# Masks and sums of a state scan moved from GpSimd to ScalarE and VectorE, and a depthwise convolution that begins at the first tile of queries

## The chip, the cores and the metric

The kernel runs on one core of a Trainium2 chip, as one program. The core has TensorE (PE in the profile; its weight loads are PEld), VectorE (DVE), ScalarE (ACT), GpSimd (POOL) and SyncE (SP, which here issues DMAs). The metric is the device time of one execution in microseconds (us), less being better. Before the change the median of three runs is 3319.76 us, from 3314.33 to 3324.03. All arithmetic is float32; the large products are made as three products of a high and a low part (fp32r), so that each costs three matmuls.

## The reference

One inference step of a hybrid backbone with two layers. The tokens are 128 of a context and 1024 of a noisy latent, 1152 in all, each of 1024 numbers. Per layer one input projection feeds three mixers that stand side by side: attention with compressed keys (8 heads), a bidirectional state scan (4 heads of 64, chunks of 128 tokens), and a convolution module. Then come the output projection, and a gated feed-forward part.

```python
h = rmsnorm(x, g_mix) * (1 + sc1) + sh1
comb = h @ w_in                            # [ q_c | ckv | krope | z x B C dt | conv a b ]

# state scan, both directions, chunk by chunk
acs = cumsum(dt * a)
seg = exp(where(lower, acs[l] - acs[s], -inf))
y_diag = einsum('bclhn,bcshn,bhcls,bcshp->bclhp', cf, bf, seg, x * dt)
y_off = einsum('bclhn,cbhpn,bhcl->bclhp', cf, h_in, exp(acs))
ssm = rmsnorm((y_fwd + y_bwd + ssd_d * xs) * silu(z))

# convolution module
g = a * sigmoid(b)
g = dwconv(g, cm_conv_w) + cm_conv_b       # 31 taps, each channel by itself
conv = silu(layernorm(g))                  # over the channels

attn = softmax(q @ k.T * scale) @ v
x = x + g1 * (concat([attn, ssm, conv]) @ w_out)
x = x + g2 * (silu(h2 @ w_gate) * (h2 @ w_up)) @ w_down
```

## The kernel before

Tokens are worked in three chunks of 384, which are nine tiles of 128. Within a layer the stages follow each other in this order: the projection of the scan's inputs; the scan's states (`ssd_states`); the convolution module's projection and gate (`conv_in`, which writes `glu`, 256 channels in two tiles of 128 by 1167 useful columns); the token-major projection of q_c, ckv and krope (`token_major`, with `token_tail` for norms, rotary keys and transposes); the scan's outputs (`ssd_out`); `latents`, `prep_k`, `prep_v`, `prep_r` and `prep_q`, which make keys, values and queries; attention; the output projection; the feed-forward part. A string of letters (L737) interleaves `conv_in`, `ssd_states`, `token_major`, `ssd_out` and `latents`, so their instructions lie among each other.

The program names no order of its own between engines beyond that: a scheduler reorders the instructions when the program is built, and then every engine works off its queue in a fixed order and waits where an operand or a buffer isn't ready. What stands behind a waiting instruction on its engine waits too.

`ssd_out` (L475 to L553) makes nine chunks' outputs. For a chunk, two masks of 128 by 128 (`M_in`, one for each direction) are multiplied by the four heads' columns of dt (L492, two GpSimd instructions of 128 by 512 in tiles of the tag E), added on VectorE (L78), and multiplied by the product of C and B from PSUM (L501). The exponents come from four masked tiles `mv` (L508; three buffers), two from the high part of dt·a on VectorE and two from its low part on GpSimd, of which TensorE makes `db` (L510); ScalarE takes the exponential (L512). Then come TensorE's `yb` (L523), the product D·x (L526) and, from chunk 1 on, two sums of `y` with the states' part `of` (L78). These three are on GpSimd for chunks 0 to 4 and on VectorE for chunks 5 to 8.

The long convolution (`conv_taps`, L863 to L873) is all on GpSimd: for each of two accumulators a first tap (L868) and 30 further taps, each a product (L871) and a sum (L78) of 128 by 1167. It needs only `glu`. A one-column copy on GpSimd (L517) from the scan's last exponentials into `ct`, the taps' scratch tile, stands ahead of them, so that they begin when chunk 8 of the scan has its exponentials. In the program text three taps are drawn per tile of queries.

Attention goes over four pairs of heads and nine tiles. From the 26th tile on, one step of `conv_norm` is drawn per tile: TensorE sums the two accumulators over channels (L881), VectorE centres (L885), ScalarE squares (L889), TensorE sums squares (L896), and so on. `load_w` brings a weight tile, rounds it to its high part on ScalarE (L84) and makes the low part `wl` on GpSimd (L81) in one of four buffers; those of the output projection stand in GpSimd's queue among layer 1's taps.

Of the kernel before, what the change touches and what calls it, by code (L numbers as in the profile page):

```python
# [53 lines left out]
def build(tc, nc, ap, dbg=None):  # L54
# [99 lines left out]
    def spread(r, dg, tag):  # L154
        """[128 tokens, 3] -> a PSUM bank with r of each token on every partition."""
        dg = dg.rearrange("p (a b) -> p a b", a=3)
        V.tensor_mul(dg, ident.unsqueeze(1).to_broadcast([128, 3, 128]),
                     r.unsqueeze(2).to_broadcast([128, 3, 128]))
        b = bank(tag)
        PE.matmul(b[:, :CH], ones, dg.rearrange("p a b -> p (a b)"), start=True, stop=True)  # L160
        return b

# [1 line left out]
    KO = (0, 4, 1, 5, 2, 6, 3, 7)  # L164

    def adas(rounds, stage=None, ahead=2):
        """128 columns of each of a round's four quarters at a time; loads run ahead of the products"""
        stage = stage or wp
        steps = [(l, r, q, k) for l, r in rounds for q in range(4) for k in range(0, KD, 2)]
        loads = []  # L170
        m = None
        for n in range(len(steps) + ahead):
            if n < len(steps):
                l, r, q, k = steps[n]
                loads.append(stage.tile([128, 1024], F32, tag="ws", name="ws", bufs=ahead + 1))
                Q.dma_start(loads[-1], ap["w_ada"][l, r, q, k // 2])
            if n >= ahead:
                l, r, q, k = steps[n - ahead]
                st = loads.pop(0)
                if k == 0:  # L180
                    m = sm.tile([128, 128], F32, tag="ms", name="ms", bufs=2)
                b = bank("A")
                for kk in range(2):
                    for j in range(4):
                        o = 512 * kk + 128 * j
                        PE.matmul(b[32 * j:32 * j + 32, :128], cond[:, k + kk, :], st[:, o:o + 128],
                                  start=kk == 0, stop=kk == 1)
                if k:
                    add_to(V, m, b[:, :128], m)
                else:  # L190
                    copy(m, b[:, :128])
                if k == KD - 2:
                    ada_end(l, r, q, m)
            yield
# [25 lines left out]
    def norm_r(x, p, sqs=None):  # L220
        """1 / rms of the chunk's tokens on every partition; sqs: room for all squares, summed on TensorE"""
# [79 lines left out]
    for c in (1, 2):  # L301
        # a load that would only hold up the modulation's goes behind them
        V.tensor_copy(X[c][:, 0, 0:1], modT[0][:, c + 1, 0:1])
        Q.dma_start(X[c], ap["xT"][:, c])
# [5 lines left out]
    for l in range(L):  # L310
# [6 lines left out]
        def h_terms(c, w):  # L317
            """stationary weights [k, cols], moving h chunk"""
            hh, hl = H[c]
            return [(w[0][:, 128 * k:128 * k + 128], w[1][:, 128 * k:128 * k + 128], hh[:, k], hl[:, k])  # L320
                    for k in KO]

        # ================= in projection: x, B, C of the scan =================
# [17 lines left out]
        for c in range(NC3):  # L341
# [34 lines left out]
        # lowest: what the attention's first tiles can take over soonest  # L376
# [6 lines left out]
        # ================= state-space scan =================  # L383
        # dt = softplus(.), log1p(e) = 2 atanh(e / (2 + e))
# [89 lines left out]
        def ssd_out():  # L474
# [12 lines left out]
            for c in range(9):  # L487
                o = xcol(c)
                # dt of the pairs of tokens in each direction's range
                W = [tmp(512, "E", 4).rearrange("p (h t) -> p h t", h=4) for _ in range(2)]  # L490
                for d in range(2):
                    G.tensor_tensor(W[d], M_in[d].unsqueeze(1).to_broadcast([128, 4, 128]),  # L492
                                    v4(dt)[:, d, c, :].unsqueeze(2).to_broadcast([128, 4, 128]), ALU.mult)
                add_to(V, W[0], W[1], W[0])
                W = W[0]
# [7 lines left out]
                # a direction's exponents are 0 outside of its range  # L503
                db = bank("A")
                for d in range(2):
                    for i, (dd, en) in enumerate(((dah, V), (dal, G))):
                        mv = tmp(512, "mv", 3, F32R).rearrange("p (h t) -> p h t", h=4)
                        en.tensor_tensor(mv, M_in[d].unsqueeze(1).to_broadcast([128, 4, 128]),  # L508
                                        v4(dd.bitcast(F32))[:, d, c, :].unsqueeze(2).to_broadcast([128, 4, 128]), ALU.mult)
                        PE.matmul(db, M_sr[d], mv.rearrange("p h t -> p (h t)"), start=d + i == 0, stop=d + i == 2)  # L510
# [3 lines left out]
                if c == 8:  # L514
                    # the long convolution's products would hold up the scan on this engine
                    lat["ct"] = r4t("ct")
                    G.tensor_copy(lat["ct"][:, 0:1], E[:, 0, 0:1])  # L517
# [7 lines left out]
                e = G if c < 5 else V  # L525
                e.tensor_tensor(y.rearrange("p (h q) -> p h q", h=4), xst[:, c].rearrange("p (h q) -> p h q", h=4),  # L526
                                dsum.unsqueeze(2).to_broadcast([128, 4, 64]), ALU.mult)
                V.tensor_add(y, y, yb[:, :256])
                if c:
# [7 lines left out]
                    for d in range(2):  # L537
                        add_to(e, y, of[:, d].rearrange("p h q -> p (h q)"), y)
# [16 lines left out]
        # ================= in projection: conv module =================  # L555
# [28 lines left out]
        def latent(c):  # L584
            """chunk c's query latent (high and low part, halves), key latent (high and low part), rotary key"""
# [35 lines left out]
        def token_tail(c, tns, ss):  # L621
            # rotary key part
# [57 lines left out]
        def latents():  # L680
            # cached keys
# [60 lines left out]
        # ================= attention =================  # L742
# [42 lines left out]
        class Tile_:  # L785
            """one tile of queries of a pair of heads"""
# [6 lines left out]
            def scores(self, j):  # L793
                """exp of a head's scores, less their maximum, and the sums"""
# [27 lines left out]
            def attend(self):  # L822
# [25 lines left out]
                # divide by the sums  # L848
# [14 lines left out]
        def conv_taps():  # L863
            ct = lat["ct"]
# [10 lines left out]
        def conv_norm(c):  # L875
            """layer norm over channels and silu of chunk c"""
# [68 lines left out]
        # ================= out projection, residual, norm 2 =================  # L945
# [36 lines left out]
        # ================= feed-forward =================  # L982
# [21 lines left out]
        def finish(c):  # L1004
            """what follows the layer for chunk c: the next layer's first norm, or the final norm"""
# [13 lines left out]
            # nothing is left to overlap with  # L1019
# [7 lines left out]
        def apply(c, rs):  # L1027
            """the final norm's scale for chunk c"""
# [70 lines left out]
def layouts(i):  # L1099
    """the arrays of setup_inputs, laid out for the program"""  # L1100
# [80 lines left out]
```

## Time and profile before

| what | value |
|---|---|
| median of 3 runs | 3319.76 us |
| profiled execution, its span from first to last instruction | 3325.1 us |
| granted TensorE clock, mean over the span | 0.967 |
| TensorE busy | 3123.8 us (94%) |
| VectorE busy | 1856.9 us (56%) |
| ScalarE busy | 1081.1 us (33%) |
| GpSimd busy | 1183.7 us (36%) |

The profile gives of the profiled execution its span alone, no time of its own; the span lies 5.3 us above the median of the three runs and 1.1 us above the longest of them. Busy times are sums over instructions. A matmul's end is modelled, so a busy TensorE need not be at its peak; of the clock, 1.0 is full speed. In a row of the timeline, "[48.58 <-ACT wh L84]" is the engine's idle time before the instruction and what ended it.

### The profile page before, as it was taken

The page shows a single profiled execution, that of the slowest core. Times are in us where ns is not written, and L with a number is a line of the kernel's source. Part 1 is how long each engine was busy: PE and PEld are TensorE (multiplying, and loading weights), DVE is VectorE, ACT ScalarE, POOL GpSimd, SP SyncE. Part 2 cuts the span into 40 slices and gives each one's busy share as a digit, 9 for nine tenths or more (in the row PEclk, how much of TensorE's full clock was granted, in tenths as well). Part 3 has the DMA queues.
Part 4 walks back from the last instruction along what each step waited for, and adds up shares of the span by engine and source line. Part 5 has one row for each costly group of instructions (what it writes and reads, how often), then busy time and mean ns, then how long its engine had stood idle before and what let it go on. Part 6 is the DMA issues. An engine that isn't in the chain of part 4 may idle for free. (4 is left out here: it accounts for less than half of the span.)

```text
span 3325.1 us, 50558 instructions
## 1 busy us (share of the span) xinstructions
PE 3123.8 (94%) x20610; PEld 2900.9 (87%) x20610; DVE 1856.9 (56%) x3811; ACT 1081.1 (33%) x2461; POOL 1183.7 (36%) x699
## 2 busy tenths in 40 slices
PE   6995799999999999999999957999999999999998
PEld 5974667779999999999999746777899999999997
DVE  6779876663733333333386798777463333333335
ACT  4433455563411111111143334667431111111113
POOL 2457994012412112111233579672232212112112
PEclk7997899999999999999999978999999999999998
DMA  6100333334111111111121010000311111111111
GB/s 233 54 24 31 115 113 122 125 132 146 29 48 45 45 39 45 45 39 39 51 100 54 24 49 18 11 17 30 137 39 39 45 45 45 45 39 45 45 32 58
DMA packets 67000, 202.36 MB, mean 61 GB/s; under 512 B 7888, under 2 KB 25424, under 8 KB 65232
## 3 DMA queue, kind: packets, MB, share of 16 engines
q1 hardware_dynamic: 63456, 194.02, 17.5%
q10 hardware_dynamic: 3312, 5.11, 0.4%
q8 instruction: 162, 2.65, 0.3%
q14 instruction: 70, 0.57, 0.1%
HBM read 177.44 MB, written 21.66 MB: 60 GB/s over the span
## 5 line engine op out<-in xcount | busy, mean ns | idle before, releaser
L81 POOL TENSOR_TENSOR wl<-ws,wh 128x1024 fp32r<-128x1024 f32 x164 | 399.1, 2440 | 1581.0 <-ACT wh L84 1508.5
L103 PE MATMUL psA<-hh,wh 128*128 128x384 f32 x2496 | 836.6, 337 | 4.4 <-ACT hh L270 2.7
L104 PE MATMUL psA<-hl,wh 128*128 128x384 f32 x2496 | 837.5, 336 | 0.4 <-DVE hl L271 0.4
L105 PE MATMUL psA<-hh,wl 128*128 128x384 f32 x2496 | 837.5, 336 | 0.0
L103 PEld LDWEIGHTS psA<-hh,wh 128*128 128x128 f32 x2496 | 471.4, 189 | 8.5 <-ACT hh L270 3.9
L104 PEld LDWEIGHTS psA<-hl,wh 128*128 128x128 f32 x2496 | 471.6, 189 | 2.2 <-DVE hl L271 1.1
L105 PEld LDWEIGHTS psA<-hh,wl 128*128 128x128 f32 x2496 | 471.3, 189 | 0.3
L998 DVE TENSOR_TENSOR fs<-fs,psA 128x384 f32<-128x384 f32 x132 | 72.9, 554 | 666.5 <-PE psA L105 657.6
L78 POOL TENSOR_TENSOR acc<-ct,acc 128x1167 f32<-128x1167 f32 x120 | 326.5, 2720 | 9.8
L84 ACT ACTIVATE wh<-ws 128x1024 fp32r<-128x1024 f32 (+1 forms) x178 | 184.5, 1049 | 414.7 <-PE psA L104 197.4
L997 ACT ACTIVATE fs<-psA 128x384 f32<-128x384 f32 x132 | 63.8, 485 | 655.6 <-PE psA L105 655.6
L1051 DVE SCALAR_TENSOR_TENSOR x<-psT,mod,x 128x384 f32<-128x384 f32 (+1 forms) x320 | 157.7, 513 | 198.6 <-PE psT L105 198.6
L811 ACT ACTIVATE P<-psA,mx 128x384 f32<-128x384 f32 (+1 forms) x400 | 224.1, 571 | 132.8 <-DVE mx L809 87.8
L806 DVE TENSOR_REDUCE mx<-psA 128x1 f32<-128x384 f32 (+1 forms) x400 | 209.0, 540 | 78.2 <-PE psA L105 75.7
L1051 DVE SCALAR_TENSOR_TENSOR x<-psA,mod,x 128x384 f32<-128x384 f32 (+2 forms) x384 | 186.8, 513 | 53.4 <-PE psA L105 46.9
L1001 DVE TENSOR_TENSOR fl<-fs,fh 128x384 fp32r<-128x384 f32 x132 | 167.5, 1270 | 65.7 <-ACT fh L84 65.7
L843 PE MATMUL psV<-pt,vv 128*64 128x128 f32 x2336 | 191.5, 285 | 5.4 <-DVE pt L837 2.8
L832 PE MATMUL psT<-cst,P 128*128 128x128 f32 x1168 | 193.9, 287 | 2.4 <-DVE mod L203 1.0
L104 PE MATMUL psA<-fl,wh 128*128 128x384 f32 x576 | 193.2, 335 | 0.0
L105 PE MATMUL psA<-fh,wl 128*128 128x384 f32 x576 | 193.0, 335 | 0.0
L103 PE MATMUL psA<-fh,wh 128*128 128x384 f32 x576 | 189.9, 337 | 2.7 <-DVE fs L998 2.7
L103 PE MATMUL psA<-K,q 128*128 128x384 f32 (+1 forms) x400 | 160.6, 402 | 28.2 <-ACT P L811 21.5
(267 smaller groups left out, 6020.1 us busy)
## 6 DMA issues: line engine op xcount, KB each, us to landing
ws<-w_ada SPq DMA_DIRECT2D x96, 512.0 KB, 3.4
ws<-w_gate SPq DMA_DIRECT2D x44, 512.0 KB, 3.6
ws<-w_up SPq DMA_DIRECT2D x44, 512.0 KB, 3.5
ws<-w_down SPq DMA_DIRECT2D x44, 512.0 KB, 3.5
x<-xT SPq DMA_DIRECT2D x6, 1536.0 KB, 7.8
ws<-w_fm SPq DMA_DIRECT2D x16, 512.0 KB, 3.4
ws<-w_out SPq DMA_DIRECT2D x16, 512.0 KB, 3.6
mf<-mixed SPq DMA_DIRECT2D x18, 384.0 KB, 5.7
```

What stands on the lines that cost most here:

```text
L78: eng.tensor_tensor(out, a, b, ALU.add)
L81: eng.tensor_tensor(out, x, hi.bitcast(F32), ALU.subtract)
L84: S.activation(out, x, AF.Copy)
L103: PE.matmul(out, sh, mh, start=i == 0, stop=False)
L104: PE.matmul(out, sh, ml, start=False, stop=False)
L105: PE.matmul(out, sl, mh, start=False, stop=i == n - 1)
L806: V.reduce_max(mx[:, b:b + 1], b0[:, :w], axis=AX.X)
L811: S.activation(pr[:, CH * b:CH * b + w], bs[b][:, :w], AF.Exp, bias=mx[:, 3:4], scale=SCALE, accum_out=sl[:, 3 * j + b:3 * j + b + 1])
L832: PE.transpose(tb[:, 256 * u + 128 * j:256 * u + 128 * j + 128], prs[j][:, 128 * (a + u):128 * (a + u) + 128], ident)
L843: PE.matmul(ob[64 * j:64 * j + 64, :128], vv[:, kt, 64 * h:64 * h + 64], pt[:, 256 * u + 128 * j:256 * u + 128 * j + 128], start=kt == kts ...
L1001: V.tensor_sub(fl[:, sl], sg, fh[:, sl].bitcast(F32))
L1051: V.scalar_tensor_tensor(X[c][:, m, a:b], b0[:, a:b], modT[l][:, 40 + m, s:s + 1], X[c][:, m, a:b], ALU.mult, ALU.add)
```

## The change

In `ssd_out` the masks with dt become four ScalarE copies of 128 by 128 with dt as scale (direction 0), and four VectorE instructions that multiply and add (direction 1). The two low-part tiles `mv` are made by four ScalarE copies each. The product D·x and its sums are on VectorE for all chunks. The copy that stood ahead of the long convolution now reads the first tile of queries instead of the scan's last exponentials. The rest of the diff drops comments.

```diff
-                W = [tmp(512, "E", 4).rearrange("p (h t) -> p h t", h=4) for _ in range(2)]
-                for d in range(2):
-                    G.tensor_tensor(W[d], M_in[d].unsqueeze(1).to_broadcast([128, 4, 128]),
-                                    v4(dt)[:, d, c, :].unsqueeze(2).to_broadcast([128, 4, 128]), ALU.mult)
-                add_to(V, W[0], W[1], W[0])
-                W = W[0]
+                W = tmp(512, "E", 4).rearrange("p (h t) -> p h t", h=4)
+                for h in range(4):
+                    S.activation(W[:, h], M_in[0], AF.Copy, scale=v4(dt)[:, 0, c, h:h + 1])
+                for h in range(4):
+                    V.scalar_tensor_tensor(W[:, h], M_in[1], v4(dt)[:, 1, c, h:h + 1], W[:, h], ALU.mult, ALU.add)
...
-                    for i, (dd, en) in enumerate(((dah, V), (dal, G))):
+                    for i, dd in enumerate((dah, dal)):
                         mv = tmp(512, "mv", 3, F32R).rearrange("p (h t) -> p h t", h=4)
-                        en.tensor_tensor(mv, M_in[d].unsqueeze(1).to_broadcast([128, 4, 128]),
-                                        v4(dd.bitcast(F32))[:, d, c, :].unsqueeze(2).to_broadcast([128, 4, 128]), ALU.mult)
+                        if i:
+                            for h in range(4):
+                                S.activation(mv[:, h], M_in[d], AF.Copy, scale=v4(dd.bitcast(F32))[:, d, c, h:h + 1])
+                        else:
+                            V.tensor_tensor(mv, M_in[d].unsqueeze(1).to_broadcast([128, 4, 128]),
...
-                if c == 8:
-                    # the long convolution's products would hold up the scan on this engine
-                    lat["ct"] = r4t("ct")
-                    G.tensor_copy(lat["ct"][:, 0:1], E[:, 0, 0:1])
...
-                e = G if c < 5 else V
-                e.tensor_tensor(y.rearrange("p (h q) -> p h q", h=4), xst[:, c].rearrange("p (h q) -> p h q", h=4),
+                V.tensor_tensor(y.rearrange("p (h q) -> p h q", h=4), xst[:, c].rearrange("p (h q) -> p h q", h=4),
...
-                        add_to(e, y, of[:, d].rearrange("p h q -> p (h q)"), y)
+                        add_to(V, y, of[:, d].rearrange("p h q -> p (h q)"), y)
...
         def conv_taps():
-            ct = lat["ct"]
+            ct = r4t("ct")
+
+            G.tensor_copy(ct[:, 0:1], qs[0, 0][0][:, 0, 0:1].bitcast(F32))
```

On GpSimd in layer 1 the scan's last masks, the copy and the taps stand like this before (`E` and `mv` are the scan's tiles, `ct` the taps' scratch, `acc` an accumulator, `wl` a weight's low part):

```order
L508 TENSOR_TENSOR mv<-cst,dal 128x512
L492 TENSOR_TENSOR E<-cst,dt 128x512
L517 COPY ct<-E 128x1
L868 TENSOR_SCALAR acc_18578<-glu_16830,par 128x1167
L871 TENSOR_SCALAR ct<-glu_16830,par 128x1167
L78 TENSOR_TENSOR acc_18578<-ct,acc_18578 128x1167
L81 TENSOR_TENSOR wl<-ws,wh 128x1024
```

And the same place of the changed kernel, where the copy reads a tile `q` of queries:

```order
L447 TENSOR_TENSOR of<-xst,wd 128x512
L81 TENSOR_TENSOR wl<-ws,wh 128x1024 x3
L865 COPY ct<-q_18708 128x1
L869 TENSOR_SCALAR acc_18758<-glu_16920,par 128x1167
L869 TENSOR_SCALAR acc_19856<-glu_17349,par 128x1167
L872 TENSOR_SCALAR ct<-glu_16920,par 128x1167
L78 TENSOR_TENSOR acc_18758<-ct,acc_18758 128x1167
```

The scan's instructions are gone from this queue, and the copy waits for queries. Further on, before had 43 pairs of product and sum, a `wl`, 17 pairs and two more `wl`; the changed kernel has 35 pairs, a `wl`, 17 pairs with the product of the next, a second `wl`, that pair's sum and seven pairs, and a third `wl`.

On TensorE, still in layer 1, the sums over channels of the first chunk stand at the end of attention. Before:

```order
L843 MATMUL psV<-pt,vv 64x128 x4
L854 MATMUL psT<-dl,ones 64x128 x2
L843 MATMUL psV<-pt,vv 64x128 x2
L832 MATMUL psT<-cst,P 128x128 x2
L881 MATMUL psA<-acc_19676,ones 128x128
L881 MATMUL psA<-acc_18578,ones 128x256
L881 MATMUL psA<-acc_19676,ones 128x256
L832 MATMUL psT<-cst,P 128x128 x2
L103 MATMUL psA<-K_18228,q_21643 128x128
```

And in the changed kernel (`lsq` are the squares, L897 is L896 of before):

```order
L105 MATMUL psA<-K_18407,q_21828 128x384
L882 MATMUL psA<-acc_19856,ones 128x128
L882 MATMUL psA<-acc_18758,ones 128x256
L882 MATMUL psA<-acc_19856,ones 128x256
L897 MATMUL psT<-ones,lsq 128x1 x3
L831 MATMUL psT<-cst,P 128x128 x2
L853 MATMUL psT<-dl,ones 64x128 x2
```

The sums that read the second accumulator moved back to where the sum of squares stood before (from row 9765 to 9797 of TensorE's list), and the sum of squares now stands directly behind them.

## Rows read from the trace of the kernel before

**Rows 1.** Stretches: from:to, us, engines' busy us (instructions), granted PE clock, DMA share, GB/s.

```profile
160.00:277.00 117.00, 111.59 (x600) 92.61 (x600) 91.48 (x208) 36.81 (x93) 62.96 (x58) 0.97 0.08 25
277.00:352.00 75.00, 29.77 (x132) 23.23 (x131) 71.56 (x94) 24.86 (x62) 65.42 (x31) 0.67 0.19 60
1938.00:2009.00 71.00, 28.98 (x135) 23.70 (x135) 68.75 (x96) 25.52 (x63) 62.33 (x29) 0.66 0.20 68
352.00:541.00 189.00, 175.69 (x1812) 132.18 (x1813) 142.40 (x328) 94.63 (x286) 180.82 (x91) 0.96 0.34 120
541.00:750.00 209.00, 205.32 (x2072) 159.53 (x2070) 143.94 (x419) 125.97 (x346) 9.43 (x5) 0.99 0.37 126
```

**Rows 2.** VectorE's groups of instructions, 277.4 to 352 us: busy us, mean ns.

```profile
L647 DVE SCALAR_TENSOR_TENSOR tn<-tn,ry,rows 128x256 f32<-128x256 f32 x6 | 7.8, 1303 | 0.0
L582 DVE TENSOR_TENSOR K<-krr,K 64x512 fp32r<-64x512 f32 x2 | 5.3, 2642 | 0.1
...
L733 DVE TENSOR_TENSOR K<-psA,K 64x512 fp32r<-64x512 f32 x2 | 1.4, 686 | 0.0
L582 DVE TENSOR_TENSOR lat<-bt,lat 128x128 fp32r<-128x128 f32 x1 | 1.2, 1247 | 0.0
```

**Rows 3.** VectorE lines over the whole span: duration in ns, shortest/median/longest, first to last start.

```profile
L647 DVE SCALAR_TENSOR_TENSOR tn<-tn,ry,rows x18: 468/480/2949, 240.8 to 1991.9; 128x256 f32<-128x256 f32 x18
...
L582 DVE TENSOR_TENSOR lat<-bt,lat x2: 273/760/1247, 290.1 to 1953.9; 128x128 fp32r<-128x128 f32 x2
```

**Rows 4.** GpSimd's taps over the whole span, columns as in rows 3.

```profile
L871 POOL TENSOR_SCALAR ct<-glu,par x120: 1242/1302/2477, 271.4 to 2252.9; 128x1167 f32<-128x1167 f32 x120
...
L78 POOL TENSOR_TENSOR acc<-ct,acc x120: 2639/2684/3085, 272.7 to 2254.2; 128x1167 f32<-128x1167 f32 x120
```

**Rows 5.** ScalarE's timeline, first queries of either layer: start us, us, instruction [idle before].

```profile
346.34 0.48 ACT L84 ACTIVATE q<-psA 64x384 fp32r<-64x384 f32 x1 [0.89 <-PE psA L105]
...
2004.69 0.48 ACT L84 ACTIVATE q<-psA 64x384 fp32r<-64x384 f32 x1 [2.55 <-PE psA L105]
```

**Rows 6.** ScalarE's groups over the whole span.

```profile
L780 ACT ACTIVATE q<-qr,cst 64x384 fp32r<-64x384 f32 x48 | 29.5, 614 | 11.6 <-PE psA L105 5.9 <-DVE qr L78 4.7
...
L610 ACT ACTIVATE y<-tn 128x128 f32<-128x128 f32 x18 | 5.6, 312 | 0.4
...
L84 ACT ACTIVATE K<-krr 64x384 fp32r<-64x384 f32 x8 | 4.2, 522 | 0.2
```

**Rows 7.** VectorE's products of 128 by 128 and the masks' sum, columns as in rows 3.

```profile
L645 DVE SCALAR_TENSOR_TENSOR tn<-tn,ry,rows x18: 334/346/2805, 239.8 to 1991.6; 128x128 f32<-128x128 f32 x18
...
L78 DVE TENSOR_TENSOR E<-E x18: 673/680/1524, 147.9 to 1927.5; 128x512 f32<-128x512 f32 x18
```

**Rows 8.** GpSimd's timeline, last taps of layer 1.

```profile
2182.90 2.37 POOL L81 TENSOR_TENSOR wl<-ws,wh 128x1024 fp32r<-128x1024 f32 x1 [48.58 <-ACT wh L84]
2185.25 1.55 POOL L871 TENSOR_SCALAR ct<-glu,par 128x1167 f32<-128x1167 f32 x1
...
2254.24 2.68 POOL L78 TENSOR_TENSOR acc<-ct,acc 128x1167 f32<-128x1167 f32 x1
2266.82 2.37 POOL L81 TENSOR_TENSOR wl<-ws,wh 128x1024 fp32r<-128x1024 f32 x1 [9.90 <-PE psA L105]
```

**Rows 9.** TensorE's timeline, sums over channels in both layers.

```profile
638.30 1.48 PE L881 MATMUL psA<-acc,ones 128*128 128x128 f32 x8
...
2267.98 1.25 PE L881 MATMUL psA<-acc,ones 128*128 128x128 f32 x6
...
2278.94 0.83 PE L896 MATMUL psT<-ones,lsq 128*128 128x1 f32 x6
```

**Rows 10.** TensorE's timeline after an idle stretch.

```profile
246.47 0.69 PE L103 MATMUL psA<-wh,hh 128*128 128x416 f32 x1 [2.44 <-DVE E L501]
246.96 0.55 PE L104 MATMUL psA<-wl,hh 128*128 128x416 f32 x1
...
251.93 0.35 PE L105 MATMUL psA<-wh,hl 128*128 128x416 f32 x1
```

More of the change, by code (lines that the diff above doesn't have):

```diff
@@ L505, in ssd_out @@
                 for d in range(2):
-                    for i, (dd, en) in enumerate(((dah, V), (dal, G))):
+                    for i, dd in enumerate((dah, dal)):
                         mv = tmp(512, "mv", 3, F32R).rearrange("p (h t) -> p h t", h=4)
-                        en.tensor_tensor(mv, M_in[d].unsqueeze(1).to_broadcast([128, 4, 128]),
-                                        v4(dd.bitcast(F32))[:, d, c, :].unsqueeze(2).to_broadcast([128, 4, 128]), ALU.mult)
+                        if i:
[3 more added lines that the diff above has]
+                            V.tensor_tensor(mv, M_in[d].unsqueeze(1).to_broadcast([128, 4, 128]),
+                                            v4(dd.bitcast(F32))[:, d, c, :].unsqueeze(2).to_broadcast([128, 4, 128]),
+                                            ALU.mult)
                         PE.matmul(db, M_sr[d], mv.rearrange("p h t -> p (h t)"), start=d + i == 0, stop=d + i == 2)
```

## The prediction

> **What bounds the kernel now.** I read the table of stretches first [rows 1]: look for one in which TensorE, which is 94% of the span busy, is not. From 277 to 352 us, between the end of the token-major projection and the start of attention, TensorE has 29.8 us of 75, at a granted clock of 0.67, while VectorE is busy for 71.6; 1938 to 2009 reads alike (29.0 of 71, VectorE 68.8). In the scan before it, 160 to 277, TensorE has 111.6 of 117 and ScalarE 36.8. So VectorE sets the end of these two stretches, and the question is why it is so slow there.
>
> The grouping of VectorE's instructions says it [rows 2]: the same 64x512 subtraction takes 2642 ns where both inputs lie in SBUF (K<-krr) and 686 ns where one is PSUM (K<-psA). The statistics of a line say the same in time [rows 3]: L647 has a median of 480 ns and a longest of 2949. GpSimd's taps last 1302 and 2684 ns [rows 4] and run through these stretches (GpSimd 65.4 of 75). A VectorE instruction that needs SBUF alone lasts about as long as the tap beside it. That is the cost which the change touches.
>
> **The gate of the taps.** Before, the first product of a tap is at 271.4 us [rows 4]. Afterwards the copy ahead of the taps waits for the first queries, whose high half ends at 346.34 + 0.48 = 346.8 and 2004.69 + 0.48 = 2005.2 by before's clock [rows 5]; call these B0 and B1. Of each stretch only the last 5 us then still lie beside taps. Seventeen groups of VectorE that read only SBUF have 59.0 us in the stretch of layer 0 (the first and the last are in rows 2). At the shortest duration of each line they need 17.3 (L647: 6 x 0.468 = 2.8 instead of 7.8; lat<-bt 0.27 instead of 1.25 [rows 3]): 41.7 us less, and VectorE needs 29.9. With its 3.4 us of idle time and about 5 for the hops between engines that it covers today, I make the stretch 38 us instead of 75; less 2.5 for the part beside taps the gain is 34.5. For layer 1 I scale by VectorE's busy time, 68.8/71.6: 33 us, taken as 32.5. Bounds: no less than 0, no more than what TensorE leaves, 75 - 29.8 = 45 and 71 - 29 = 42. What is late next is TensorE itself with ScalarE's 24.9 us of evictions: that is why I don't take the bounds.
>
> **Masks and sums.** GpSimd loses its scan instructions, the busy 63 us of 160 to 277 in the main. ScalarE gains 12 copies of 128x128 per chunk, 108 per layer. No such instruction with a scale column stands in before. L610 has the shape without a column of scales, 0.312 us; L780 against the copy K<-krr of the same shape, 0.614 - 0.522, puts 0.09 on the column [rows 6]. So 0.40 each, bounds 0.31 and 0.61: 43 us per layer (33 to 66). ScalarE goes from 36.8 to 80 of 117. VectorE gains 36 instructions at L645's 0.346 and loses 9 sums at 0.68 [rows 7], and gains 5 products and 8 sums of 128x256 at about L647's 0.480 [rows 3]: 12.5 - 6.1 + 6.2 = +12.6 us per layer, with 25 us idle in the scan and the taps gone. Both lie beside TensorE's projections, which fill 111.6 of 117. If that cover holds, the most to be won is TensorE's idle 5.4 us; the masks come from engines that wait less, and I take +3 per layer. If it fails, all 43 us stand on the path.
>
> [...]
>
> **The taps beside attention.** From 352 to 541, with taps, TensorE is busy for 93.0% of the stretch; from 541 to 750, without, for 98.2% [rows 1]. A microsecond of taps that moves into attention so costs 0.053. In layer 0 taps fill 194 us of attention today (346.8 to 541) and 252 afterwards: 60 pairs at about 4.16 and the first taps. That is +58, 3 us lost. In layer 1 about +29 outside of the wait below: 1.5 us.
>
> **A new wait in layer 1.** GpSimd's queue there has low parts of output-projection weights among the taps, which wait for buffers that attention's own preparation frees: the second ends its wait at 2182.90, which is B1 + 177.7, and the third at 2266.82, B1 + 261.6 [rows 8]. In the changed order 35 pairs stand ahead of the first of these. With 17 pairs in 2185.25 to 2256.92, 4.2 us each, they are done at B1 + 149.6; GpSimd waits 28 us to B1 + 177.7, needs 2.4 for the weight, 71.4 for 17 pairs and 1.3 for one product: B1 + 252.8. The next weight holds it until B1 + 261.6 + 2.4 = 264.0. The sum left over and seven pairs, 2.7 + 7 x 4.2 = 32.1, end at B1 + 296. TensorE wants the second accumulator at the place that L896 has today, 2278.94 [rows 9] less the sums that now stand there, about B1 + 273. It stands still for 23 us, and everything on its queue behind. The sum of squares is now directly behind, so centring, squares and their sum add about 2.5; after an idle stretch the clock is low for a while (0.55 instead of 0.35 us per matmul, 246.47 to 251 [rows 10], some 2.3 us). Some 2 us of the later sums are caught up. I take 26 us; bounds 0 (the weights' buffers come free earlier, as attention's head runs sooner) and 35 (two more weights' waits). In layer 0 no such weight stands between: the taps end at B0 + 252, and TensorE reaches the sums at 638.30 [rows 9], B0 + 291.5. It doesn't wait.
>
> **Sum.** Layer 0: 34.5 + 3 - 3 = 34.5. Layer 1: 32.5 + 3 - 1.5 - 26 = 8. Together 42.5 us off the profiled 3325.1, 3282.6. That execution stands 5.3 above the median of the runs; on the median's level it is 3277. I forecast 3276. The kernel's measurement can tell about 0.3%, 10 us, from no change: faster means under 3309.8.
>
> **Rivals.**
>
> A, the forecast, 3276, with 3256 to 3296 as its own range: 54%.
>
> B, no new wait in layer 1: 3277 - 26 = 3251. For it: the wait rests on a chain of five estimates, and the taps' pace would have to be only 10% faster, or the buffer freed 20 us sooner. Against it: both releases hang on TensorE's own progress, which shifts with B1. 15%.
>
> C, ScalarE becomes the bound of the scan. The mechanism: db waits for eight copies (3.2 us) in the three mv buffers, and the exponential stands behind them in the same queue, so that each chunk's masks add to the chain of chunks instead of lying beside projections. All of it is 9 x 4.8 = 43 us per layer, 86 in both: 3276 + 86 = 3362, slower. From a share of 0.5 the gain is used up, and above 0.61 the kernel is measurably slower. For it: TensorE's 2.44 us of waiting on L501 [rows 10], which the masks feed, shows that the chain can reach TensorE. Against it: ScalarE has 80 us idle, the masks depend on dt alone, known before the scan's outputs begin, so only buffers hold them. A quarter on the path (3298) 13%, about half (3319) 4%, more (to 3362) 5%.
>
> D, the stretch is not VectorE's: the hops of TensorE, ScalarE and VectorE through K, v and the rotary queries have a length of their own, at a low clock, and it shrinks by 15 us each instead of 34 and 32. Then 3277 + 36.5 = 3313. For it: TensorE has the clock at 0.67 there, and at that rate a chain of dependent steps isn't shortened by faster VectorE work alone. Against it: VectorE idles for only 3.4 of 75 us. 9%, a little over half of it faster than 3309.8.
>
> **How the numbers follow.** Faster: A, B, the quarter of C, and 5 of D's 9: 0.87. Same: the half of C and the rest of D, 0.08. Slower: the rest of C, 0.05. The range has to reach B's 3251 with its own spread and the quarter of C with part of D: 3242 to 3307, leaving out B's lower end, C from a half up and the larger part of D, under 2 in 10.
>
> **What would show it.** Between the last token-major product and the first queries, K<-krr at about 0.55 to 0.7 us and a stretch of about 38 us prove the first term; K<-krr short in an unchanged stretch means D. In GpSimd's timeline of layer 1 a wait of some 28 us ahead of a wl, and TensorE idle ahead of the L882 sums of the first chunk for about 23, prove the wait; no idle time there means B. ScalarE near 80 us in the scan's stretch and TensorE still above 105 of it prove the cover; a scan longer than 117 us, with TensorE waiting on db or on E behind ScalarE, means C. If the taps still start ahead of the first queries, nothing of the first term holds.

## The result and the profile after

The changed kernel takes 3274.2 us (median of 4 runs, 3269.32 to 3282.06) where the kernel before takes 3320.36 on the same chip: a ratio of 0.9861, 95% interval 0.9844 to 0.9879. That is 1.4% faster, and the whole interval lies below 1. The forecast was 3276. The profiled execution has a span of 3280.3 us, 44.8 less than before's.

The stretches of the changed kernel, in the columns of [rows 1]; the second and third lie between the last token-major product and the first queries.

```profile
160.00:277.00 117.00, 111.64 (x611) 93.98 (x609) 81.66 (x254) 69.58 (x200) 13.49 (x12) 0.97 0.14 44
270.50:310.70 40.20, 28.75 (x130) 23.65 (x130) 32.46 (x96) 21.84 (x59) 2.24 (x1) 0.75 0.31 99
1898.00:1938.20 40.20, 29.02 (x131) 23.93 (x130) 34.44 (x97) 22.67 (x61) 4.76 (x2) 0.75 0.34 108
310.70:560.00 249.30, 227.70 (x2304) 173.14 (x2304) 189.61 (x421) 123.27 (x367) 238.61 (x121) 0.97 0.34 114
560.00:750.00 190.00, 184.87 (x1804) 144.48 (x1801) 125.10 (x357) 114.93 (x307) 25.04 (x15) 1.00 0.45 158
```

The same stretch of before, cut at the same events, with GpSimd busy for 60.6 us of it:

```profile
277.70:347.00 69.30, 28.75 (x128) 22.67 (x128) 65.92 (x87) 23.76 (x60) 60.60 (x29) 0.66 0.19 61
```

TensorE does the same 28.75 us of work in 40.2 us instead of 69.3, and VectorE is busy for 32.5 instead of 65.9. The line that stood for the waits, K<-krr (shortest, median, longest in ns), lasts 0.55 to 0.69 us now, where it was up to 3.0 before (first line):

```profile
L582 DVE TENSOR_TENSOR K<-krr,K x12: 541/994/3015, 284.5 to 1988.9; 64x384 fp32r<-64x384 f32 x8, 64x512 fp32r<-64x512 f32 x4
L581 DVE TENSOR_TENSOR K<-krr,K x12: 549/555/689, 278.1 to 1921.2; 64x384 fp32r<-64x384 f32 x8, 64x512 fp32r<-64x512 f32 x4
```

The first queries come at 310.70 and 1938.16, which answers to [rows 5], and GpSimd's copy begins the taps right behind them:

```profile
310.22 0.48 ACT L84 ACTIVATE q<-psA 64x384 fp32r<-64x384 f32 x1 [2.99 <-PE psA L105]
1937.68 0.48 ACT L84 ACTIVATE q<-psA 64x384 fp32r<-64x384 f32 x1 [3.51 <-PE psA L105]
```

```profile
310.76 0.19 POOL L865 COPY ct<-q 128x1 f32<-128x1 f32 x1 [38.02 <-ACT q L84]
310.94 2.94 POOL L869 TENSOR_SCALAR acc<-glu,par 128x1167 f32<-128x1167 f32 x2
```

And the new wait in layer 1. GpSimd's timeline, which answers to [rows 8]:

```profile
2101.28 2.41 POOL L81 TENSOR_TENSOR wl<-ws,wh 128x1024 fp32r<-128x1024 f32 x1 [12.87 <-ACT wh L84]
...
2193.66 2.37 POOL L81 TENSOR_TENSOR wl<-ws,wh 128x1024 fp32r<-128x1024 f32 x1 [16.88 <-PE psA L105]
...
2225.61 2.64 POOL L78 TENSOR_TENSOR acc<-ct,acc 128x1167 f32<-128x1167 f32 x1
```

TensorE's timeline at the sums over channels, which answers to [rows 9]:

```profile
2208.29 0.33 PE L105 MATMUL psA<-K,q 128*128 128x384 f32 x1
2228.31 2.50 PE L882 MATMUL psA<-acc,ones 128*128 128x128 f32 x6 [19.69 <-POOL acc L78]
2233.45 1.41 PE L897 MATMUL psT<-ones,lsq 128*128 128x1 f32 x6 [2.64 <-DVE lsq L78]
```

The last sum of the taps ends at 2228.25, and TensorE goes on 0.06 us later, having stood for 19.7 us.

### The profile page after: what moved, and what is told of

Its sections match the earlier page's. It is cut to its first block, busy times and chain, and to the rows that moved or that the text cites. A ratio compares the mean times of both kernels' runs of the same rounds, so it can differ in the third digit from the quotient of the medians.

```text
span 3280.3 us, 50736 instructions
## 1 busy us (share of the span) xinstructions
PE 3120.5 (95%) x20610; PEld 2899.1 (88%) x20610; DVE 1754.9 (53%) x3891; ACT 1144.7 (35%) x2677; POOL 1070.2 (33%) x601
## 5 line engine op out<-in xcount | busy, mean ns | idle before, releaser
L1002 DVE TENSOR_TENSOR fl<-fs,fh 128x384 fp32r<-128x384 f32 x132 | 167.5, 1270 | 65.9 <-ACT fh L84 65.9
```

The source lines that it names most:

```text
L1002: V.tensor_sub(fl[:, sl], sg, fh[:, sl].bitcast(F32))
```

## The experiments

**The gate alone.** The kernel before, with this edit:

```diff
-                if c == 8:
-                    lat["ct"] = r4t("ct")
-                    G.tensor_copy(lat["ct"][:, 0:1], E[:, 0, 0:1])
...
-            ct = lat["ct"]
+            ct = r4t("ct")
+            G.tensor_copy(ct[:, 0:1], qs[0, 0][0][:, 0, 0:1].bitcast(F32))
```

> The kernel before with one edit: the copy ahead of the taps reads the first queries (the scan's masks and sums stay on GpSimd). Theory 1, the taps slow VectorE's SBUF-only work wherever they run beside it, and the gate alone moves them out: the stretch between the last token-major product and the first queries shrinks in layer 0 from 69 to about 40 us (K<-krr about 0.55 us), in layer 1 from 66 to about 40; the scan before it keeps its length; the wait for the taps in layer 1 (about 22 us) and 4 us of attention are lost as in the changed kernel. 3320 - 29 - 26 + 4 + 22 = 3291 us. Theory 2, the gain came from taking the scan's work off GpSimd: the stretches stay above 60 us, and with the wait in layer 1 the time is 3320 to 3345 us.

Measured: 3280.64 us, ratio 0.9877 (0.9864 to 0.9891). The stretches:

```profile
276.30:310.70 34.40, 25.59 (x126) 21.25 (x124) 29.38 (x84) 21.11 (x57) 2.98 (x2) 0.80 0.40 126
1905.10:1942.20 37.10, 28.44 (x126) 23.77 (x124) 29.96 (x84) 22.29 (x59) 5.40 (x3) 0.72 0.38 127
```

Theory 2 falls: with the scan's work still on GpSimd the stretches are 34.4 and 37.1 us, and the ratio to before is 0.9877 where the changed kernel's is 0.9861, with intervals that overlap. So nearly all of the gain is the gate's. The stretches are even shorter than in the changed kernel. In layer 0 the first queries come at 310.7 in both; the changed kernel ends its token-major products 5.8 us earlier (270.5 against 276.3) and then needs 5.8 us more. My 3291 was too high because I had taken the scan's 7 and 9 us as a gain of the masks that this kernel would lack.

**The masks alone.** The changed kernel with the old copy from the scan's last exponentials in place of the one from the queries.

> The changed kernel with the old gate: masks and sums on ScalarE and VectorE, the taps begin after the last exponentials of the scan. Theory 1: the scan with the token-major products is 7 us (layer 0) and 9 us (layer 1) shorter, the stretch behind it keeps about 65 us, there is no wait for the taps in layer 1: 3320 - 16 = 3304 us. Theory 2: most of the gain is here, 3285 us or less.

Measured: 3330.59 us, ratio 1.0027 (1.0017 to 1.0037): 9 us slower than before. Both theories missed. The stretch behind the token-major products, in the columns of the stretches above:

```profile
270.80:350.00 79.20, 32.39 (x133) 24.99 (x132) 74.25 (x98) 22.58 (x60) 63.75 (x32) 0.61 0.18 57
```

The projections do end at 270.9 instead of 277.7, but the scan's rest, now with more work for VectorE, falls into the stretch and waits for the taps there; the first queries come at 349.1, 2.2 us later than before, and in layer 1 2.8 us later. Where the rest of the 9 us goes was not traced. In this kernel the masks' move does not pay while the taps run in the stretch.

**No weight among the taps.** The changed kernel with one word more:

```diff
-        wo = [load_w(ap["w_out"][l, m]) for m in range(4)]
+        wo = [load_w(ap["w_out"][l, m], V) for m in range(4)]
```

> The changed kernel with the low parts of the first four output-projection weights on VectorE, so that no weight stands among the taps on GpSimd. Theory 1: the taps of layer 1 end some 255 us after the first queries, about 2194, TensorE reaches the sums over channels at about 2208 and doesn't wait; the 19.7 us of idle time and 2.6 behind it go: 3274 - 21 = 3253 us (3249 to 3257). Rival: the weights wait on VectorE for the same buffers and hold up attention's maxima behind them, by up to 17 + 13 us: 3265 to 3285 us.

Measured: 3254.15 us, ratio 0.9799 (0.9786 to 0.9812). GpSimd's taps of layer 1 have nothing between them and end at 2186.4; TensorE's weight loads (PEld) for the sums don't wait:

```profile
2183.71 2.68 POOL L78 TENSOR_TENSOR acc<-ct,acc 128x1167 f32<-128x1167 f32 x1
```

```profile
2202.30 1.02 PEld L882 LDWEIGHTS psA<-acc,ones 128*128 128x128 f32 x6
2208.63 1.35 PEld L897 LDWEIGHTS psT<-ones,lsq 128*128 128x128 f32 x6 [5.31 <-DVE lsq L78]
```

Theory 1 stands: the wait for the taps is gone. That the time is the one forecast is in part luck. Of the 26.4 us between the two profiled spans some 9 were won before the queries of layer 1 (1929.4 against 1938.2), which it had not spoken of; against that the sums of squares still wait 5.3 us.

**The gate and the weights, without the masks.** The kernel before with the edits of the first and third experiment.

> The kernel before with the new gate and with the first four output-projection weights' low parts on VectorE; the scan's masks and sums stay on GpSimd. Theory 1, the masks' move is worth nothing: 3254 us as with it, within 3 us. Rival, what they were worth (about 4 us at the first queries of layer 1) was hidden by the wait for the taps and shows when the wait is gone: 3258 to 3262 us.

Measured: 3269.46 us, ratio 0.9838 (0.9822 to 0.9853), against 0.9799 with the masks moved. By the ratios the masks' move is worth some 13 us here (0.0039 of 3320; from the two intervals I estimate 6 to 20), more than the rival gave it.

The profiles say where. In this pair the first queries of layer 1 come at 1941.0 without and 1929.4 with the masks moved, a lead of 11.7 us. In the first pair (this change against its gate alone) they come at 1942.2 and 1938.2, a lead of 4.0. Further on, in layer 1's attention, the leads are alike: the same exponential (`P<-psA`) starts at 2121.95 and 2113.81 in the first pair, and another at 2135.19 and 2127.31 in the second, 8.1 and 7.9 us. From there to a later common exponential, in the columns of the stretches above: the gate alone, the changed kernel; then this kernel, and the one with the weights on VectorE:

```profile
2121.95:2169.06 47.11, 42.66 (x360) 35.47 (x359) 33.93 (x85) 29.76 (x91) 45.11 (x23) 1.00 0.03 9
2113.81:2169.36 55.55, 48.35 (x360) 40.26 (x359) 37.43 (x85) 30.10 (x92) 53.19 (x27) 0.88 0.02 8
2135.19:2179.27 44.08, 38.35 (x304) 31.38 (x303) 32.80 (x71) 23.13 (x69) 42.18 (x22) 0.88 0.02 6
2127.31:2163.68 36.37, 34.16 (x304) 27.94 (x303) 28.90 (x71) 22.88 (x69) 34.77 (x18) 1.00 0.02 7
```

As many matmuls take 8.4 us more in the changed kernel, and 7.7 us more in this one, each time at a granted clock of 0.88 instead of 1.00. In the changed kernel a slow VectorE instruction beside a tap comes first, 2.34 us where q<-qr takes 0.60 at its shortest and 0.68 in the median of 48. The maxima for the next exponential stand behind it in VectorE's queue, and TensorE waits for that exponential:

```profile
2131.26 2.34 DVE L780 SCALAR_TENSOR_TENSOR q<-qr,cst,q 64x384 fp32r<-64x384 f32 x1
2134.95 0.69 PE L103 MATMUL psA<-K,q 128*128 128x384 f32 x1 [3.13 <-ACT P L810]
```

From 2136 to 2140 the granted clock is then 0.50, where it was 1.00 from 2131 to 2134. This kernel (the gate and the weights, without the masks) has the same wait of 3.1 us at 2145.10, and 0.50 from 2146 to 2150. So the first pair loses its lead ahead of the wait for the taps: TensorE starts its last product ahead of the sums at 2208.29 in the changed kernel and at 2208.05 with the gate alone, and then both wait for the same 19.7 us. In the second pair the lead doubles to 15.6. Some 8 us for the masks' move is what the profiles show up to these stretches, and the rest lies in them. Each kernel has one profile; whether its other executions have the low clock at the same place is not shown.

TensorE's weight load at the sums, in the kernel with the gate alone, beside 2228.30 in the changed kernel:

```profile
2228.07 1.78 PEld L878 LDWEIGHTS psA<-acc,ones 128*128 128x128 f32 x6 [20.01 <-POOL acc L78]
```

Why the lead at the queries is 11.7 us in one pair and 4.0 in the other was not settled. No run parts ScalarE's masks from the sums and products on VectorE, which moved with them.

**ScalarE's masks twice.** The changed kernel, with this:

```diff
-                for h in range(4):
+                for h in (0, 0, 1, 1, 2, 2, 3, 3):
                     S.activation(W[:, h], M_in[0], AF.Copy, scale=v4(dt)[:, 0, c, h:h + 1])
...
-                            for h in range(4):
+                            for h in (0, 0, 1, 1, 2, 2, 3, 3):
                                 S.activation(mv[:, h], M_in[d], AF.Copy, scale=v4(dd.bitcast(F32))[:, d, c, h:h + 1])
```

> The changed kernel with each of ScalarE's 128x128 mask copies issued twice (108 more of 0.39 us per layer, 42 us each). Theory 1, ScalarE's masks lie beside TensorE's projections: the time grows by less than 10 us, to 3274 to 3284 us. Rival C, ScalarE's masks are on the scan's path: by a quarter to all of 84 us, 3295 to 3358 us.

Measured: 3295.91 us, ratio 0.9931 (0.9918 to 0.9943), 21.7 us above the changed kernel by the medians and 23 by the ratios: a quarter of the 84 us added, the low end of the rival. The first queries come 11.6 us later in layer 0 and 18.6 later in layer 1. ScalarE in the scan's stretch:

```profile
160.00:279.50 119.50, 111.83 (x605) 92.69 (x603) 74.87 (x241) 97.42 (x299) 9.79 (x11) 0.99 0.09 29
```

At 97 of 119.5 us busy the masks come through to TensorE; at 69.6 of 117 in the changed kernel they cost nothing against GpSimd's, since the kernel with the gate alone has its first queries at the same time in layer 0. The cover was real, and less than a doubling from its end.

**The taps in free pieces.** The kernel before, with the taps cut in three:

```diff
-                    G.tensor_scalar(ct[:, :CO], glu[j][:, t:t + CO], P("cw", w0 + t), 1.0, ALU.mult, ALU.mult)
-                    add_to(G, acc[j][:, :CO], ct[:, :CO], acc[j][:, :CO])
+                    for o, e in ((0, 389), (389, 778), (778, CO)):
+                        G.tensor_scalar(ct[:, o:e], glu[j][:, t + o:t + e], P("cw", w0 + t), 1.0, ALU.mult, ALU.mult)
+                        add_to(G, acc[j][:, o:e], ct[:, o:e], acc[j][:, o:e])
```

> The kernel before with each product and sum of the taps cut into three pieces of columns (389, 389, 389), the gate as before. Theory 1, a VectorE instruction on SBUF waits for the end of the GpSimd instruction that runs: the waits fall from about 2.7 us to under 1, K<-krr of 512 columns lasts 1 to 1.5 us instead of 2.64, and the stretch between the token-major products and the first queries shrinks in layer 0 from 69 us to about 50, in layer 1 by as much: 3320 - 38 = 3282 us. If the pieces make the taps more than 10 us longer, TensorE waits for them in layer 1, up to 20 us more. Rival, both engines share what SBUF delivers, whatever the pieces: the durations and the stretch stay, 3315 to 3325 us.

Measured: 3358.43 us, ratio 1.0113 (1.0095 to 1.013). That is 38 us more than before, and both theories missed the time. The gate holds only the first piece here, so a first product of the others runs early. The stretch is 58.8 us, between the two theories, and TensorE waits 20.6 us for longer taps in layer 1:

```profile
275.00:333.80 58.80, 32.46 (x131) 24.82 (x130) 53.47 (x98) 21.86 (x59) 48.44 (x53) 0.62 0.24 77
```

**Free pieces in the faster kernel.** The same cut in the kernel with the weights on VectorE.

> The changed kernel with the output-projection weights' low parts on VectorE and the taps in three pieces of columns. Theory 1, attention loses some 5% beside taps because VectorE's instructions on SBUF wait for whole taps: with pieces of a third the loss falls to about a third, 27 us to 10: 3237 us, if the taps still end ahead of the sums. Rival, the loss doesn't hang on the length of a piece, or longer taps eat it: 3250 to 3265 us.

Measured: 3301.26 us, ratio 0.9937 (0.9917 to 0.9956), slower by some 46 us than with whole taps, though TensorE waits for no sum of taps here. The first theory's rule, a wait until the running GpSimd instruction ends, is wrong for these pieces. `dl` is the diagonal tile with the reciprocals of attention's sums, 128 by 256 from two inputs in SBUF, and takes 0.41 us at its shortest. One `dl` on VectorE's timeline, and GpSimd's timeline beside it:

```profile
352.86 13.10 DVE L849 TENSOR_TENSOR dl<-cst,sl 128x256 f32<-128x256 f32 x1
```

```profile
351.68 1.72 POOL L873 TENSOR_SCALAR ct<-glu,par 128x389 f32<-128x389 f32 x3
353.37 2.96 POOL L78 TENSOR_TENSOR acc<-ct,acc 128x389 f32<-128x389 f32 x3
356.31 1.72 POOL L873 TENSOR_SCALAR ct<-glu,par 128x389 f32<-128x389 f32 x3
358.00 2.92 POOL L78 TENSOR_TENSOR acc<-ct,acc 128x389 f32<-128x389 f32 x3
...
365.49 0.84 POOL L873 TENSOR_SCALAR ct<-glu,par 128x389 f32<-128x389 f32 x1
```

Three products and three sums follow each other with no time between them (351.68 + 1.72 = 353.40, where the next has begun at 353.37), and VectorE stands for 13.1 us, through 17 GpSimd instructions. No gap shows at the end of its wait either: it is done at 365.96, within the product that starts at 365.49 and takes 0.84 us instead of some 0.58. And most `dl` don't wait like this. Of the 72 in this trace 52 start while a piece runs; 46 of these last under 1.8 us, six last 3.3 to 16.1. What lets VectorE in early or late is not shown. Whole taps, each of which waits for the one before it, leave a gap. GpSimd in the kernel with whole taps:

```profile
334.53 2.67 POOL L78 TENSOR_TENSOR acc<-ct,acc 128x1167 f32<-128x1167 f32 x1
337.30 1.25 POOL L872 TENSOR_SCALAR ct<-glu,par 128x1167 f32<-128x1167 f32 x1
338.64 2.69 POOL L78 TENSOR_TENSOR acc<-ct,acc 128x1167 f32<-128x1167 f32 x1
```

Here 0.09 to 0.10 us lie between them, and no `dl` is longer than 2.8 us. The longest starts at 1980.77, beside a sum that ends at 1983.29, and is done 0.28 us later:

```profile
1980.77 2.80 DVE L849 TENSOR_TENSOR dl<-cst,sl 128x256 f32<-128x256 f32 x1
1980.61 2.68 POOL L78 TENSOR_TENSOR acc<-ct,acc 128x1167 f32<-128x1167 f32 x1
```

**Pieces in a chain.** The kernel before again, with all three pieces in the same columns of `ct`, so that each product waits for the sum ahead of it:

```diff
+                    for o in (0, 389, 778):
+                        G.tensor_scalar(ct[:, 0:389], glu[j][:, t + o:t + o + 389], P("cw", w0 + t), 1.0, ALU.mult, ALU.mult)
+                        add_to(G, acc[j][:, o:o + 389], ct[:, 0:389], acc[j][:, o:o + 389])
```

> The kernel before, gate as before, the taps in three pieces of 389 columns that all use the same third of the scratch tile, so that every product waits for the sum before it and every sum for its product (the run with free pieces had GpSimd's instructions end to end). Theory 1a, a VectorE instruction on SBUF gets its turn in the first gap that GpSimd's own waits leave: with a gap after each piece no wait is longer than about 1.2 us, K<-krr of 512 columns lasts 0.7 to 1.6 us, the stretch of layer 0 is 45 to 52 us instead of 69, and the longest dl is under 2 us. The taps need some 320 us instead of 252, which may make TensorE wait for them in layer 1: 3275 to 3310 us in all. Rival, VectorE's waits grow with the number of GpSimd instructions, whatever lies between: the stretch stays at 59 us or more, and single waits of several us stay.

Measured: 3306.03 us, ratio 0.9966 (0.9954 to 0.9979). The stretch of layer 0, and all of `dl` (shortest, median, longest):

```profile
276.90:325.00 48.10, 30.66 (x127) 25.20 (x127) 44.15 (x88) 22.51 (x59) 43.84 (x46) 0.68 0.31 94
```

```profile
L850 DVE TENSOR_TENSOR dl<-cst,sl x72: 413/500/1224, 331.8 to 2331.7; 128x256 f32<-128x256 f32 x72
```

And `dl` with the free pieces of the run before (that run has the new gate; with free pieces and the gate of this one the longest is 16.1 us too):

```profile
L849 DVE TENSOR_TENSOR dl<-cst,sl x72: 408/594/16090, 317.7 to 2329.8; 128x256 f32<-128x256 f32 x72
```

The same work in the same pieces, and the longest `dl` goes from 16.1 us to 1.2 with the gaps, which are 0.09 to 0.11 us here (between the pieces from 289.57 to 295.49 us). Theory 1a stands in the stretch, in `dl` and in the whole time. It missed the size of the wait for the taps in layer 1, which is 52.2 us and eats most of the gain, and K<-krr, which reaches 2.28 us where 0.7 to 1.6 were expected. That happens twice, at 281.97 and 1903.15, both times beside a weight's low part of 2.5 us on GpSimd and not beside a piece.

**No taps.** The kernel with the weights on VectorE; the 60 products and sums per layer are left out, so it computes less.

> The changed kernel with the output-projection weights' low parts on VectorE, and with the 60 products and sums of each layer's taps left out (the convolution has its first tap alone). Theory 1: each of some 500 us of taps beside attention costs 0.053 us: 3254 - 27 = 3227 us. Rival, attention's lower TensorE share in its first part has other causes (its first tiles): 3245 us or more.

Measured: 3199.19 us, ratio 0.963 (0.9616 to 0.9645), 55 us below the kernel with them. Theory 1 had half of it. The first stretch with the nearest number of matmuls, without and with taps:

```profile
309.00:530.00 221.00, 218.34 (x2308) 168.85 (x2308) 148.37 (x422) 123.41 (x371) 2.69 (x2) 1.00 0.39 129
```

```profile
309.00:560.00 251.00, 230.82 (x2318) 175.85 (x2317) 190.25 (x424) 125.36 (x374) 240.27 (x121) 0.96 0.34 114
```

The same matmuls take 30 us more beside taps, in which VectorE has 42 us more busy time for as many instructions and TensorE's granted clock is 0.96 instead of 1.00. A microsecond of taps so costs 30/252 = 0.12 us on the average of all taps in a layer.

**`dl` on ScalarE.** The kernel with the weights on VectorE, and this:

```diff
-                V.tensor_tensor(dl, ident.unsqueeze(1).to_broadcast([128, 2, 128]),
-                                sl[:, 6:8].unsqueeze(2).to_broadcast([128, 2, 128]), ALU.mult)
+                for j in range(2):
+                    S.activation(dl[:, j], ident, AF.Copy, scale=sl[:, 6 + j:7 + j])
```

> The changed kernel with the output-projection weights' low parts on VectorE, and with the diagonal dl of attention (two copies of 128x128 per tile with the sums' reciprocals as scale) on ScalarE instead of VectorE. Theory 1: attention loses to the taps what VectorE waits for them; dl has 26 x (0.99 - 0.41) = 15 us of that per layer, which goes: 3254 - 30 = 3224 us. Rival, VectorE's waits for dl lie beside other work, or ScalarE's 0.78 us more per tile in the chain to the output take their place: 3248 to 3262 us.

Measured: 3242.3 us, ratio 0.9777 (0.9762 to 0.9791): 12 us below the kernel without this edit by the medians, 7 by the ratios to before on either chip, and 13.6 by the profiled spans. 30 were expected, and the rival gave none. So VectorE's time on `dl` is part of attention's loss, and part of it lay beside other work. That the waits alone are the gain is not shown, since `dl`'s own 0.41 us left VectorE as well. Its median is the lowest of the kernels that compute everything.

**Two pieces in a chain on top of it.** The taps in halves of 584 and 583 columns, both in the first half of `ct`; in a second kernel eight taps of the second accumulator are one VectorE instruction each.

> The run with dl on ScalarE and the weights' low parts on VectorE, with the taps in two pieces of columns that use the same half of the scratch tile, so that a gap lies behind every piece. Theory 1a: a wait on VectorE is at most 1.5 us instead of 2.8; of the 43 us that this kernel still stands above the one without taps some 15 go; a pair takes about 4.54 us instead of 4.16, the taps 272 us, and TensorE waits for them for about 9 us in layer 1: 3236 us (3228 to 3242). Rival, the longer taps eat what the shorter waits give: 3242 us or more.

> The same, and eight taps of the second accumulator in each layer are one VectorE instruction each, ahead of GpSimd's. GpSimd needs 36 us less per layer, so TensorE doesn't wait in layer 1; VectorE has 16 x 1.3 = 21 us more in attention, where it idles for a quarter of the time, and holds GpSimd for as long: 3227 us (3220 to 3236). Rival, VectorE's eight products wait for GpSimd and hold up the maxima behind them: 3242 us or more.

Measured: 3254.71 us, ratio 0.9805 (0.978 to 0.983), and 3246.15 us, 0.9779 (0.9758 to 0.98). Layer 0 from 309 to 560 us, with halves and with whole taps:

```profile
309.00:560.00 251.00, 247.64 (x2645) 191.47 (x2647) 172.52 (x455) 155.04 (x468) 232.35 (x209) 1.00 0.38 129
```

```profile
309.00:560.00 251.00, 236.59 (x2421) 181.32 (x2422) 172.93 (x418) 143.13 (x430) 240.27 (x122) 0.97 0.35 118
```

The halves let 224 more matmuls through, at a clock of 1.00. But a pair takes 4.8 us instead of the 4.54 I had estimated, and TensorE waits for the taps of layer 1 for 34.0 us. The second kernel has no such wait, but has 2457 matmuls in the same stretch, at a clock of 0.97. Its VectorE instructions are themselves 1.42 to 2.62 us long; that they take back what the halves gave is argued and not shown. Neither is faster than the run before them, and the second's ratio, 0.9779, can't be told from its 0.9777.

## Why the prediction was right, step by step

The whole was right: 3276 forecast, 3274.2 measured. Cut at the events that the prediction named, with times of the profiled executions:

| step | forecast | measured |
|---|---|---|
| layer 0, scan and stretch up to the first queries | -37.5 | -36.1 (346.82 to 310.70) |
| attention and the rest of layer 0 | +3 | +4.1 |
| layer 1, scan and stretch | -35.5 | -35.0 |
| layer 1 from its queries on (wait, attention) | +27.5 | +22.2 |
| sum | -42.5 | -44.8 |

**The gate of the taps.** Right, and for the reason given: moving the gate alone shortens layer 0's stretch to 34.4 us and brings the first queries 36.1 us forward, where I had 34.5 for this term; K<-krr is at 0.54 to 0.69 us there. The price of a VectorE instruction at its shortest in the trace was the right price for one without taps beside it: K<-krr took 541 ns at its shortest before and 542, with a median of 556, with the gate alone; lat<-bt 273 before and 276 to 279. Rival D (the hops have a length of their own) fell: the stretch came to 40.2, not to 54 (69.3 less 15).

**Why VectorE waited.** "About as long as the tap beside it" was right for these taps, which leave a gap of about 0.1 us behind each: the longest `dl` ends 0.28 us behind the sum that ran beside it. It is no rule for GpSimd streams without gaps, where one instruction stood through 17 of GpSimd's. There `dl` was not done when the GpSimd instruction that ran at its start had finished, 0.54 us on (353.40 less 352.86), but 13.1 us on. What decides how long it stands was not shown.

**Masks and sums.** Here the step was wrong in its parts. I took 3 us per layer from TensorE's idle time in the scan. In layer 0 the projections ended 5.8 us earlier than with the gate alone, and the stretch behind them was 5.8 us longer: a shift and no gain. In layer 1 it was 4 us at the queries and 8 in mid-attention, of which nothing was left when TensorE came to the sums, because of the stretch at the granted clock of 0.88. That my sum came out is owed in part to luck: the other errors were small and of the other sign. A mask cost 390 ns on ScalarE (L492, median of 72), beside the 400 that I took from rows. These masks came from GpSimd, and no run gives them to VectorE instead. Their move, with the sums', is within the interval of no change here and some 13 us of gain once the wait was gone, and twice as many masks would have cost 22. Rival C's mechanism was near and did not come true at this load.

**The taps beside attention.** Forecast 3 us and measured 4.1 in layer 0, but the term was mis-sized: a microsecond of taps costs 0.12 us and not 0.053. I had compared TensorE's busy share of two stretches of one kernel that do different work, and left out that its clock was 0.96 in one and 0.99 in the other [rows 1]. With 0.12 the 58 us moved would have been some 7; the trace gives 4.1, so the average is not the price of these 58 either.

**The new wait in layer 1.** Right in place and mechanism, 19.7 us instead of 23. GpSimd waited 12.9 us ahead of the first weight and 16.9 ahead of the second, where I had 28 and 9. The first weight was released at 163 us behind the queries instead of 178, the second at 255 instead of 262, and the taps ended at 290 instead of 296. The 2.6 us of wait at the sum of squares were forecast at 2.5. With the 19.7 that makes 22.3, as much as the table has for layer 1 from its queries on. Taking the weights off GpSimd removed the wait, so B had the mechanism of a better kernel and not of this one.

## What to carry to other kernels

Compare an instruction's longest and shortest duration in one trace before counting an engine as busy: VectorE's 65.9 us of busy time in the stretch before were some 30 of work (29.4 with the gate alone) and the rest waiting for GpSimd, and the cure was to start GpSimd's long work later, not to make it less. Work that is moved in time then needs the end of its new place checked, too: a third of what the two stretches gave was lost to one wait behind weights that happened to share GpSimd's queue, and one argument took it back.

## What the hardware showed that I had not expected

A VectorE instruction with its inputs in SBUF stood behind a GpSimd stream without gaps for much longer than the instruction it met: 13.1 us at 352.86, and 16.1 at the longest, in the runs with free pieces. Most did not: 46 of 52 `dl` that met such pieces lasted under 1.8 us. With gaps of about 0.1 us between dependent GpSimd instructions no `dl` lasted much longer than the instruction beside it: 1.2 us with thirds, 2.8 with whole taps. So shorter GpSimd instructions made the kernel some 46 us slower where they were independent, and let more matmuls through in layer 0's attention where each waited for the last. TensorE's granted clock from 309 us on in layer 0 was lower where a VectorE instruction lasted longer on average (busy time over instructions): 0.96 at 0.45 us, beside whole taps; 0.97 at 0.41, beside whole taps with `dl` on ScalarE and beside halves with eight taps on VectorE (176.48 us, 432 instructions); 1.00 at 0.38 and 0.35, beside halves and without taps. Whether the one makes the other was not shown. In two kernels it was 0.50 for at least 4 us right behind a stand of 3.1 us, which in the changed kernel followed a VectorE instruction of 2.34 us beside a tap.
